# A second place for the state space matrices, and their loads one group ahead

## The chip, the cores and the metric

The kernel runs on one core of a Trainium2 chip. The metric is the device time of one execution, in microseconds (us); the value given for a kernel is the median of its runs. Five engines matter here: TensorE (PE in the profile, its weight loads PEld), VectorE (DVE), ScalarE (ACT), GpSimd (POOL), and SyncE, whose queue (SPq) issues all the DMAs of this kernel, in order.

## The reference, cut to what matters

Two transformer blocks run one after the other on 512 tokens. The second block has two branches from one input projection: an attention branch with compressed, selected and windowed keys, and a state space branch (S5). Only the latter is touched:

```python
def s5_mixer(u, a_re, a_im, log_dt, b_re, b_im, c_re, c_im, d_skip):
    ...
    lam_bar = jnp.exp(lam * dt)
    b_bar = ((lam_bar - 1.0) / lam)[..., None] * lax.complex(b_re.astype(f32), b_im.astype(f32))
    ...
        bu = jnp.einsum('btgc,gpc->btgp', u_chunk.astype(jnp.complex64), b_bar)
        a = jnp.broadcast_to(lam_bar, bu.shape)
        a_cum, b_cum = lax.associative_scan(binop, (a, bu), axis=1)
        s = a_cum * carry[:, None] + b_cum
        y = jnp.real(jnp.einsum('gcp,btgp->btgc', c_mat, s))
    ...
    return y + d_skip.astype(f32) * uf
```

The input u (512 channels in 32 groups of 16) goes through a complex linear recurrence per group and comes back as y. Then y goes through gelu and a gate (glu), and is added to the attention branch by the output projection.

## The kernel before, in words

**The matrices.** Much earlier in the kernel, `s5_params` works the recurrence out for steps of 8 tokens and writes four tables to DRAM: `etd` (input to state), `phd` (phases of the scan), `cld` (state to output) and `tmd` (input to output inside a step). The tokens are then 64 steps of 8.

**The state space stage.** `state_space()` goes over four groups `qb` of 8 channel groups each. `Xs[qb]` holds the inputs of group `qb`, read back from the DRAM tile `ud` to which the projection of u was written (four stores, L1536; the four reads are L1561). For each group there are two halves:

- `states(qb)` loads ET and PH (L1592, L1593), multiplies ET with the inputs on TensorE (L1600, 32 small matmuls in the trace), and makes the states S on VectorE: a rotation by PH, two scans, and a rotation back (L1604 to L1622).
- `loads(qb)` loads CL (two DMAs, L1585) and Tm (L1586). The output half (L1632 to L1642) multiplies Tm with the inputs and CL with the states (L1636, L1637), in two banks of PSUM named tp, copies the result over the inputs (L1640) and stores it to `yd` (L1643).

**Places.** ET, CL and Tm have one place each in SBUF, PH and S have two. A load into a place waits until the last instruction that reads the former contents is done. CL, Tm and ET are 512 KB each, PH is 256 KB, each `Xs[qb]` is 256 KB.

**The order in the program.** `state_space` is a generator. Its steps are woven by hand with those of the rest: the projection `tk1` of the compressed keys (`unit`), and then, in `sides`, the compression of keys and then of values (`cmp_keys`, `cmp_values`) on one side, and `state_space` followed by `kv_tiles` (norm, rotation and transposition of the selected keys, `ks` with the low part `ksl`, and the values `vs`) on the other; between them come the steps of a queue `todo` with the projections `tk2` (queries) and `tk3` (window keys). In program order, `states(qb + 1)` stands before the output half of group qb, and `loads(qb + 1)` behind it.

**What sets the order on the engines.** The program order is a priority only. When the kernel is built, a planner goes through the instructions with estimated times, and puts each one on its engine's queue when its inputs and its place are free by the estimate. On the chip each queue then runs in that order; where an estimate was too short, the engine stands still. So SPq is a sequence in which a DMA that waits for its place holds up those behind it.

**Weights.** Each weight tile is loaded raw (`wraw`, L198, three places), cast on ACT to its high part (`whi`, L208), and subtracted on POOL to its low part (`wlo`, L212); a product is three matmuls (L177 to L179). The compression's weights go the same way (`exraw`, L1788, and `ex`).

Of the kernel before, what the change touches and what calls it, by code (L numbers as in the profile page):

```python
# [13 lines left out]
FT = mybir.dt.float32  # L14
FR = mybir.dt.float32r
# [9 lines left out]
T = 512  # L25
# [102 lines left out]
def turns(*gens):  # L128

    gens = list(gens)  # L130
    while gens:
        for g in list(gens):
            if next(g, gens) is gens:
                gens.remove(g)
            else:
                yield
# [14 lines left out]
def tile_hybrid(ctx: ExitStack, tc: tile.TileContext, I, out):  # L151
    nc = tc.nc
# [355 lines left out]
    with tc.manual_schedule(engines={mybir.EngineType.DVE, mybir.EngineType.Activation, mybir.EngineType.PE}):  # L508
# [68 lines left out]
        for c0, n in ((0, 512), (512, 128)):  # L577
            p = s_ps()
# [138 lines left out]
    for j in range(4):  # L717
        if j < 3:
            paired = index_queries(j + 1)
        st = i_pairs[j]  # L720
# [4 lines left out]
        for i in (1, 2, 3):  # L725
            wd = acc_w[i]
            for e in range(2):
                h = 2 * j + e
                s = (s_ps, tp_ps)[e if j else 0]()
# [93 lines left out]
    for pr in range(2):  # L823
        p = tp_ps()
# [150 lines left out]
    for h in range(4):  # L975
# [39 lines left out]
        while n <= 256:  # L1015
            if n == 1:
                near_weights()
            elif n <= 64:
                s, r = s_ps(), 128 - n
# [6 lines left out]
            elif n == 128:  # L1026
                s = s_ps()
# [4 lines left out]
            else:  # L1032
                s = s_ps()
# [23 lines left out]
        p = tp_ps()  # L1057
# [3 lines left out]
        p = tp_ps()  # L1061
# [100 lines left out]
    L = [small(f"L{i}", (9, 16)) for i in range(2)]  # L1162
# [191 lines left out]
    etd = dr.tile([4, 128, 1024], FT, name="etd")  # L1354
    cld = dr.tile([4, 1024, 128], FT, name="cld")
    phd = dr.tile([4, 128, 512], FT, name="phd")
# [180 lines left out]
    for t in range(NT):  # L1537
        x = XT[:, t]
# [17 lines left out]
    ps5 = sts.enter_context(tc.tile_pool(name="ps5", bufs=1, side="right"))  # L1556
    by_group = lambda v: v.rearrange("(g c) (i j) -> (c i) g j", c=16, i=8)

    Xs = [ps5.tile([128, 8, 64], FT, name=f"X{qb}") for qb in range(4)]
    for qb in range(4):  # L1560
        nc.sync.dma_start(Xs[qb], by_group(ud)[:, 8 * qb:8 * qb + 8])  # L1561

    def cm2(o, a, b, t, conj=False):

# [9 lines left out]
    def state_space():  # L1574

        def st(name, shape, bufs=1):
            return ps5.tile([128] + list(shape), FT, tag=name, bufs=bufs, name=name)


        def loads(qb):  # L1580

            CL, Tm = st("CL", (4, 2, 128)), st("Tm", (8, 128))
            clv = cld[qb].rearrange("(i q e p) x -> i p q e x", i=2, q=4, e=2)
            for i in range(2):
                nc.sync.dma_start(CL[64 * i:64 * i + 64], clv[i])  # L1585
            nc.sync.dma_start(Tm, tmd[qb].rearrange("(g c) (t x) -> (c t) g x", c=16, t=8))  # L1586
            return CL, Tm

        def states(qb):

            ET, PH = st("ET", (4, 2, 128)), st("PH", (2, 4, 64), 2)
            nc.sync.dma_start(ET.rearrange("p q i x -> p (q i x)"), etd[qb])  # L1592
            nc.sync.dma_start(PH.rearrange("p i q j -> p (i q j)"), phd[qb])  # L1593

            bu = tp_ps()
            for q in range(4):
                for e in range(2):
                    for i in range(2):
                        c = i * 256 + q * 64
                        nc.tensor.matmul(bu[64 * e:64 * e + 64, c:c + 64], ET[:, q, i, 64 * e:64 * e + 64],  # L1600
                                         Xs[qb][:, 2 * q + e], start=True, stop=True)

            R8 = st("R8", (4, 64))
            nc.vector.tensor_copy(R8, r8[:, 4 * qb:4 * qb + 4, None].to_broadcast([128, 4, 64]))  # L1604
            nc.vector.memset(R8[:, :, 0:1], 0.0)
            W = [st(f"W{i}", (4, 64)) for i in range(2)]
            tP = t2k()[:, 0:256].rearrange("p (q j) -> p q j", q=4)
            ph = [PH[:, i] for i in range(2)]
            cm2(W, [bu[:, i * 256:(i + 1) * 256].rearrange("p (q j) -> p q j", q=4) for i in range(2)], ph, tP, True)
            for i in range(2):  # L1610
                w = W[i].rearrange("p q j -> p (q j)")
                nc.vector.tensor_tensor_scan(w, R8.rearrange("p q j -> p (q j)"), w, 0.0, op0=OP.mult, op1=OP.add)
            S = st("S", (4, 2, 64), 2)
            nc.vector.memset(S[:, :, :, 0:1], 0.0)
            tS = t2k()[:, 0:504].rearrange("p (i q j) -> p i q j", i=2, q=4)
            wv, pv = [[v[:, :, 0:63] for v in x] for x in (W, ph)]
            for i, op in enumerate((OP.subtract, OP.add)):
                nc.vector.tensor_tensor(tS[:, 0], wv[i], pv[0], op=OP.mult)
                nc.vector.tensor_tensor(tS[:, 1], wv[1 - i], pv[1], op=OP.mult)
                for e in range(2):  # L1620
                    nc.vector.tensor_tensor(S[64 * i:64 * i + 64, :, e, 1:], tS[64 * e:64 * e + 64, 0],
                                            tS[64 * e:64 * e + 64, 1], op=op)  # L1622
            return S

        S, L = states(0), loads(0)
        for qb in range(4):
            yield
            SN = states(qb + 1) if qb < 3 else None
            yield
            CL, Tm = L  # L1630

            for e in range(2):  # L1632
                ys = tp_ps()
                for q in range(4):
                    ov = ys[:, q * 64:(q + 1) * 64]
                    nc.tensor.matmul(ov, Tm[:, 2 * q + e], Xs[qb][:, 2 * q + e], start=True, stop=False)  # L1636
                    nc.tensor.matmul(ov, CL[:, q, e], S[:, q, e], start=False, stop=True)  # L1637
                    if q == 1:
                        yield
                nc.scalar.copy(Xs[qb].rearrange("p (q e) j -> p e q j", e=2)[:, e],  # L1640
                               ys[:, 0:256].rearrange("p (q j) -> p q j", q=4))
                yield  # L1642
            nc.sync.dma_start(by_group(yd)[:, 8 * qb:8 * qb + 8], Xs[qb])  # L1643
            if qb < 3:
                S, L = SN, loads(qb + 1)

    sz = {}

# [17 lines left out]
        nc.scalar.activation(t, o, AF.Tanh, scale=c)  # L1666
        nc.vector.scalar_tensor_tensor(o if dst is None else dst, t, 1.0, x, op0=OP.add, op1=OP.mult)

    p2 = ctx.enter_context(tc.tile_pool(name="p2", bufs=1))
    stp = ExitStack()  # L1670
    pp = stp.enter_context(tc.tile_pool(name="pp", bufs=1))

# [52 lines left out]
    def heads_view(x, c0, b):  # L1725
        return x[:, :, c0:c0 + 64 * b].rearrange("p t (b d) -> p t b d", d=64)

    def kv_tiles(tk, kc0, vc0, tab, name, los):

        kx = heads_view(tk, kc0, 2)  # L1730
        head_norm(kx, 2)
        yield
        rope2(kx, 2, table(tab))
        yield
        ks = []
        for g in range(2):
            k = p2.tile([128, T], FR, name=f"k{name}{g}"), los[:, g]
            kd = t2k().rearrange("p (t e d) -> p t e d", t=NT, e=2)
            for e in range(2):
                nc.scalar.copy(kd[:, :, e], kx[:, :, g])  # L1740
            yield
            p = tp_ps()
            for t in range(NT):
                nc.tensor.transpose(p[:, t * 128:(t + 1) * 128], kd[:, t].rearrange("p e d -> p (e d)"), ident)
            split(p, *k)
            ks.append(k)
        v = p2.tile([128, NT, 2, 128], FR, tag=f"v{name}", bufs=1, name=f"v{name}")
        split(heads_view(tk, vc0, 2), v[:, :, :, 0:64], v[:, :, :, 64:128])
        kvs[name] = ks, v

    kvs = {}

    ssm = state_space()
    tk1, unit = tok_proj(p2, C2["kcr"], 512, tag="tok")

# [92 lines left out]
    def cmp_values():  # L1848
        raws = {k0: cmp_raw("v", k0) for k0 in (0, 4)}
        xb = yield from blocks(128, "v", "szs")  # L1850
        yield
        p, w = yield from compress(xb, "v", "sza", raws)
        pv = p[:, 0:128].rearrange("p (k g n) -> p k g n", k=2, g=2)
        for g in range(2):
            hv = [pp.tile([128, 2, 4, 32], FR, tag=f"hv{i}", bufs=1, name=f"hv{i}") for i in range(2)]
            for k in range(2):
                split(pv[:, k, g, None].to_broadcast([128, 4, 32]), *[v[:, k] for v in hv], scale=0.5)
            yield
            o = s_ps()
            for k in range(2):  # L1860
                mm3(o[:, 0:64], [v[:, k].rearrange("p r n -> p (r n)") for v in hv], [v[:, k] for v in w],
                    k == 0, k == 1)
            vb = vcB[g]
            nc.gpsimd.memset(fl(vb), 0.0)
            for h in range(4):
                r = slice(32 * h, 32 * h + 32)
                split(o[r, 0:64], vb[r, h, 0:64], vb[r, h, 64:128])
            yield
# [10 lines left out]
    tk3, proj3 = tok_proj(pp, C2["kwn"], 256, [(C2["gbr"], 24)])  # L1879
# [4 lines left out]
        yield  # L1884
        head_norm(qv, 8)

    ksl = p2.tile([128, 2, T], FR, name="ksl")
    todo.add(proj2, q_norm(), proj3)
    side_k = cmp_keys()
    for _ in range(3):  # L1890
        some(side_k, 1)
        todo.step()
    sides = turns(chain(side_k, cmp_values()), chain(ssm, kv_tiles(tk1, 256, 384, 0, "s", ksl)))
    for i in range(16):
        some(sides, 3)
        todo.step()
# [38 lines left out]
    nc.scalar.activation(gtv, tk3[:, :, 256:280], AF.Tanh, scale=0.5)  # L1935
    nc.vector.tensor_scalar(gt, gt, 0.5, 0.5, op0=OP.mult, op1=OP.add)
    kwl = p2.tile([128, 2, T], FR, tag="tok", bufs=1, name="kwl")
    sides = turns(cmp_scores(), kv_tiles(tk3, 0, 128, 2, "w", kwl))
    todo.add(silu2("za"), silu2("zs"))
    for _ in range(12):  # L1940
        some(sides, 1)
# [200 lines left out]
```

## Time and profile before

| | |
|---|---|
| three runs | 1318.26, 1321.57, 1322.4 us; median 1321.57 |
| the profiled execution | 1316.25 us |
| its span, first to last instruction | 1314.4 us (1.85 us lie around it) |
| granted TensorE clock, mean | 0.987 |
| busy share of the span | PE 96%, PEld 79%, DVE 62%, POOL 55%, ACT 42% |
| the state space stage in the span | from the first read of the inputs (1013 us) to the last store of `yd` (1101 us) |

Every time below is in us from the span's start. A busy PE is not a PE at its peak, since matmuls are pipelined and their ends are modelled. The trace gives for each engine the time that it stood idle before an instruction, and which event ended it.

### The profile page before, as it was taken

The page shows a single profiled execution, that of the slowest core. Times are in us where ns is not written, and L with a number is a line of the kernel's source. Part 1 is how long each engine was busy: PE and PEld are TensorE (multiplying, and loading weights), DVE is VectorE, ACT ScalarE, POOL GpSimd, SP SyncE. Part 2 cuts the span into 40 slices and gives each one's busy share as a digit, 9 for nine tenths or more (in the row PEclk, how much of TensorE's full clock was granted, in tenths as well). Part 3 has the DMA queues.
Part 4 walks back from the last instruction along what each step waited for, and adds up shares of the span by engine and source line. Part 5 has one row for each costly group of instructions (what it writes and reads, how often), then busy time and mean ns, then how long its engine had stood idle before and what let it go on. Part 6 is the DMA issues. An engine that isn't in the chain of part 4 may idle for free. (4 is left out here: it accounts for less than half of the span.)

```text
span 1314.4 us, 18654 instructions
## 1 busy us (share of the span) xinstructions
PE 1257.2 (96%) x6402; PEld 1034.0 (79%) x6402; DVE 810.0 (62%) x1777; ACT 553.6 (42%) x1258; POOL 727.3 (55%) x923
## 2 busy tenths in 40 slices
PE   8999999999999999999999699999998998989998
PEld 6887887777788888888887588888778887867786
DVE  7765997676533346258667514445257747897885
ACT  5565442232243434252433113433245245658772
POOL 4545544334556465664677446566543385667673
PEclk9999999999999999999999899999999999999999
DMA  7352222221433363332875532543334965222234
GB/s 208 88 151 79 64 71 62 72 57 34 140 88 85 106 172 87 119 90 86 242 208 182 172 119 82 169 132 116 106 102 149 259 185 136 55 91 65 81 105 136
DMA packets 206140, 156.18 MB, mean 119 GB/s; under 512 B 31710, under 2 KB 179882, under 8 KB 206044
## 3 DMA queue, kind: packets, MB, share of 16 engines
q1 hardware_dynamic: 206044, 154.98, 40.3%
q8 instruction: 51, 0.84, 0.3%
q14 instruction: 45, 0.37, 0.1%
HBM read 136.58 MB, written 18.37 MB: 118 GB/s over the span
## 5 line engine op out<-in xcount | busy, mean ns | idle before, releaser
L212 POOL TENSOR_TENSOR wlo<-wraw,whi 128x256 fp32r<-128x256 f32 (+2 forms) x717 | 588.9, 851 | 471.9 <-ACT whi L208 470.4
L208 ACT CAST whi<-wraw 128x512 fp32r<-128x512 f32 (+4 forms) x390 | 212.7, 572 | 353.2 <-PE mm L178 203.2
L177 PE MATMUL mm<-hT,whi 128*128 128x512 f32 (+2 forms) x840 | 331.6, 395 | 0.0
L179 PE MATMUL mm<-hT,wlo 128*128 128x512 f32 (+2 forms) x840 | 325.6, 388 | 0.0
L178 PE MATMUL mm<-hT,whi 128*128 128x512 f32 (+2 forms) x840 | 324.7, 387 | 0.0
L179 PEld LDWEIGHTS mm<-hT,wlo 128*128 128x128 f32 x840 | 158.8, 189 | 30.7
L177 PEld LDWEIGHTS mm<-hT,whi 128*128 128x128 f32 x840 | 158.9, 189 | 28.8 <-ACT whi L208 0.2
L178 PEld LDWEIGHTS mm<-hT,whi 128*128 128x128 f32 x840 | 159.1, 189 | 27.7
L177 PE MATMUL mm<-whi,gT 128*128 128x512 f32 x176 | 71.0, 403 | 13.0 <-DVE t2k L1457 6.9
L1276 DVE TENSOR_TENSOR XT<-XT,mm 128x512 f32<-128x512 f32 x24 | 16.3, 684 | 95.9 <-PE mm L179 95.8
L178 PE MATMUL mm<-wlo,gT 128*128 128x512 f32 x176 | 70.4, 400 | 0.0
L179 PE MATMUL mm<-whi,gT 128*128 128x512 f32 x176 | 70.2, 399 | 0.0
L177 PE MATMUL mm<-whi,hT 128*128 128x512 f32 (+3 forms) x160 | 57.2, 361 | 0.2 <-ACT hT L184 0.2
L179 PE MATMUL mm<-whi,hT 128*128 128x512 f32 (+3 forms) x160 | 56.9, 356 | 0.4 <-DVE hT L185 0.4
L178 PE MATMUL mm<-wlo,hT 128*128 128x512 f32 (+3 forms) x160 | 56.3, 352 | 0.0
L185 DVE TENSOR_TENSOR pt4k<-tp,pt4k 128x512 fp32r<-128x512 f32 (+1 forms) x96 | 46.1, 485 | 15.2 <-ACT pt4k L184 14.5
L184 ACT CAST pt4k<-tp 128x512 fp32r<-128x512 f32 (+1 forms) x96 | 40.0, 421 | 32.9 <-PE tp L398 32.6
L1338 DVE SCALAR_TENSOR_TENSOR am<-aw,prm,am 128x1024 f32<-128x1024 f32 x21 | 29.6, 1408 | 37.7 <-DMA aw<-in_w_ada_dram 37.7
L177 PEld LDWEIGHTS mm<-whi,gT 128*128 128x128 f32 x176 | 33.5, 190 | 23.1 <-DVE t2k L1457 7.3
L187 ACT ACTIVATE gT<-t2k 128x512 fp32r<-128x512 f32 x22 | 13.9, 630 | 78.2 <-DVE t2k L1459 78.2
L179 PEld LDWEIGHTS mm<-whi,gT 128*128 128x128 f32 x176 | 33.6, 191 | 8.3
L178 PEld LDWEIGHTS mm<-wlo,gT 128*128 128x128 f32 x176 | 33.6, 191 | 8.0
(650 smaller groups left out, 2605.9 us busy)
## 6 DMA issues: line engine op xcount, KB each, us to landing
wraw<-in_w_in_dram SPq DMA_DIRECT2D x70, 512.0 KB, 3.8
aw<-in_w_ada_dram SPq DMA_DIRECT2D x24, 512.0 KB, 4.6
wraw<-in_w_ffn_gate_dram SPq DMA_DIRECT2D x22, 512.0 KB
wraw<-in_w_ffn_up_dram SPq DMA_DIRECT2D x22, 512.0 KB, 4.5
wraw<-in_w_ffn_down_dram SPq DMA_DIRECT2D x20, 512.0 KB, 3.8
wraw<-in_w_out_dram SPq DMA_DIRECT2D x16, 512.0 KB, 3.8
PA<-biasd SPq DMA_DIRECT2D x4, 640.0 KB, 5.9
x<-in_x_dram SPq DMA_DIRECT2D x4, 512.0 KB, 4.5
```

Of the source, the lines that this page charges most:

```text
L177: nc.tensor.matmul(o, a[0], b[0], start=first, stop=False)
L178: nc.tensor.matmul(o, a[0], b[1], start=False, stop=False)
L179: nc.tensor.matmul(o, a[1], b[0], start=False, stop=last)
L184: nc.scalar.copy(hi, p)
L185: return nc.vector.tensor_tensor(lo, p, fl(hi), op=OP.subtract)
L187: nc.scalar.activation(hi, p, AF.Copy, scale=scale)
L208: nc.scalar.copy(hi[:, d], raw[:, d])
L212: low_at[0] = nc.gpsimd.tensor_tensor(lo[:, e], raw[:, e], fl(hi[:, e]), op=OP.subtract)
L1276: nc.vector.tensor_tensor(XT[:, t, n0:n0 + 512], XT[:, t, n0:n0 + 512], o, op=OP.add)
L1338: nc.vector.scalar_tensor_tensor(am, aw, cs[:, k:k + 1], am, op0=OP.mult, op1=OP.add)
```

## The change

- ET and PH of group 0 are loaded in front of the four reads of the inputs, no longer behind them.
- ET and PH of group qb + 1 are asked for right behind the ET matmuls of group qb (they were asked for at the start of `states(qb + 1)`). The places are as before: one for ET, two for PH.
- CL and Tm of the odd groups get places of their own, in the pool p2: those of `ksl` and `vs`, which `kv_tiles` fills once the state space is done. `loads(qb + 1)` now stands right behind `states(qb + 1)`, in front of the output half of group qb.
- So that this can be, p2 is opened earlier, and `ksl` is allocated at the start of `kv_tiles`.

```diff
     Xs = [ps5.tile([128, 8, 64], FT, name=f"X{qb}") for qb in range(4)]
+    def state_loads(qb):
+        ET = ps5.tile([128, 4, 2, 128], FT, tag="ET", bufs=1, name="ET")
+        PH = ps5.tile([128, 2, 4, 64], FT, tag="PH", bufs=2, name="PH")
+        nc.sync.dma_start(ET.rearrange("p q i x -> p (q i x)"), etd[qb])
+        nc.sync.dma_start(PH.rearrange("p i q j -> p (i q j)"), phd[qb])
+        return ET, PH
+
+    first_loads = state_loads(0)
     for qb in range(4):
         nc.sync.dma_start(Xs[qb], by_group(ud)[:, 8 * qb:8 * qb + 8])
+    p2 = ctx.enter_context(tc.tile_pool(name="p2", bufs=1))
...
         def loads(qb):
-            CL, Tm = st("CL", (4, 2, 128)), st("Tm", (8, 128))
+            if qb % 2:
+                CL = p2.tile([128, 4, 2, 128], FT, tag="ksl", bufs=1, name="CL")
+                Tm = p2.tile([128, 8, 128], FT, tag="vs", bufs=1, name="Tm")
+            else:
+                CL, Tm = st("CL", (4, 2, 128)), st("Tm", (8, 128))
...
         def states(qb):
-            ET, PH = st("ET", (4, 2, 128)), st("PH", (2, 4, 64), 2)
-            nc.sync.dma_start(ET.rearrange("p q i x -> p (q i x)"), etd[qb])
-            nc.sync.dma_start(PH.rearrange("p i q j -> p (i q j)"), phd[qb])
+            ET, PH = due[qb]
...
+            if qb < 3:
+                due[qb + 1] = state_loads(qb + 1)
...
+        due = {0: first_loads}
         S, L = states(0), loads(0)
         for qb in range(4):
             yield
-            SN = states(qb + 1) if qb < 3 else None
+            if qb < 3:
+                SN, LN = states(qb + 1), loads(qb + 1)
...
             if qb < 3:
-                S, L = SN, loads(qb + 1)
+                S, L = SN, LN
...
     def kv_tiles(tk, kc0, vc0, tab, name, los):
+        los = los()
...
-    ksl = p2.tile([128, 2, T], FR, name="ksl")
...
-    sides = turns(chain(side_k, cmp_values()), chain(ssm, kv_tiles(tk1, 256, 384, 0, "s", ksl)))
+    sides = turns(chain(side_k, cmp_values()), chain(ssm, kv_tiles(tk1, 256, 384, 0, "s", lambda: p2.tile([128, 2, T], FR, tag="ksl", bufs=1, name="ksl"))))
```

## Rows read from the trace of the kernel before

**Rows 1.** The page: busy time, share of the span, instructions.
```profile
PE 1257.2 (96%) x6402; PEld 1034.0 (79%) x6402; DVE 810.0 (62%) x1777; ACT 553.6 (42%) x1258; POOL 727.3 (55%) x923
```

**Rows 2.** Busy time by stretch; in brackets instructions; last granted clock, DMA share, GB/s.
```profile
1000.00:1085.00 85.00, 84.71 (x612) 73.72 (x611) 50.68 (x108) 31.87 (x64) 44.23 (x60) 1.00 0.75 218
1016.00:1034.00 18.00, 18.00 (x117) 14.54 (x118) 8.64 (x19) 3.18 (x5) 8.75 (x13) 1.00 0.87 225
1034.00:1044.00 10.00, 9.81 (x108) 8.50 (x106) 8.58 (x20) 3.02 (x6) 4.50 (x6) 1.00 0.91 256
...
1090.00:1092.00 2.00, 2.00 (x10) 1.68 (x10) 0.47 (x2) 1.05 (x3) 0.00 (x0) 0.59 0.96 189
1092.00:1094.00 2.00, 2.00 (x11) 2.00 (x11) 1.94 (x4) 2.00 (x7) 0.79 (x2) 0.55 0.01 2
1114.00:1120.00 6.00, 5.77 (x36) 5.44 (x37) 4.83 (x9) 3.73 (x10) 3.66 (x5) 0.72 0.00 0
1120.00:1165.00 45.00, 43.09 (x226) 35.45 (x225) 40.32 (x74) 25.41 (x59) 30.09 (x31) 1.00 0.33 94
```

**Rows 3.** All waits of PE from 1005 to 1135: total us, times, longest.
```profile
PE s L178 <- POOL ex L212: 3.4, 4, 2.5
PE tp L1636 <- DMA Tm<-tmd: 2.8, 1, 2.8
PE tp L1600 <- DMA ET<-etd: 0.2, 1, 0.2
```

**Rows 4.** Timeline of PE: start, us, instruction, in brackets idle before and releaser.
```profile
1022.25 1.20 PE L1600 MATMUL tp<-X,ET 128*64 128x64 f32 x32
...
1040.62 1.17 PE L1600 MATMUL tp<-X,ET 128*64 128x64 f32 x32 [0.19 <-DMA ET<-etd]
...
1089.84 0.41 PE L1636 MATMUL tp<-X,Tm 128*128 128x64 f32 x2 [2.80 <-DMA Tm<-tmd]
...
1099.22 0.60 PE L1773 MATMUL tp<-ident,t2k 128*128 128x128 f32 x4
...
1112.15 0.33 PE L178 MATMUL s<-ex,xb 128*64 128x256 f32 x1 [2.53 <-POOL ex L212]
...
1168.51 0.33 PE L419 MATMUL s<-ks,qst 128*128 128x128 f32 x1 [4.77 <-DVE qst L188]
```

**Rows 5.** Timeline of SPq: issues of DMAs (time in the queue, waits included).
```profile
1013.14 0.39 SPq L1561 DMA_DIRECT2D X<-ud  x1
...
1017.19 0.58 SPq L1592 DMA_DIRECT2D ET<-etd  x1
...
1034.81 0.32 SPq L1592 DMA_DIRECT2D ET<-etd  x1
...
1041.45 0.62 SPq L1586 DMA_DIRECT2D Tm<-tmd  x1
1042.17 3.14 SPq L198 DMA_DIRECT2D wraw<-in_w_in_dram  x3
...
1057.55 0.64 SPq L1586 DMA_DIRECT2D Tm<-tmd  x1
1058.24 0.79 SPq L1592 DMA_DIRECT2D ET<-etd  x1
...
1084.57 0.46 SPq L1586 DMA_DIRECT2D Tm<-tmd  x1
```

**Rows 6.** Timeline of DVE, as in rows 4.
```profile
1016.41 0.39 DVE L1912 TENSOR_SCALAR nm<-cm 128x128 f32<-128x128 f32 x1 [4.60 <-DMA x2d<-XT]
1025.59 0.42 DVE L1566 TENSOR_TENSOR W<-tp,PH 128x256 f32<-128x256 f32 x1 [8.78 <-DMA PH<-phd]
...
1057.40 1.06 DVE L185 TENSOR_TENSOR vs<-tok,vs 128x512 fp32r<-128x512 f32 x1
```

**Rows 7.** Timeline of ACT, as in rows 4.
```profile
1050.89 0.62 ACT L208 CAST whi<-wraw 128x512 fp32r<-128x512 f32 x1
...
1086.19 0.41 ACT L1769 COPY t2k<-tok 128x256 f32<-128x256 f32 x1
```

More of the change, by code (lines that the diff above doesn't have):

```diff
@@ L1667, in gelu2 @@
         nc.vector.scalar_tensor_tensor(o if dst is None else dst, t, 1.0, x, op0=OP.add, op1=OP.mult)
-    p2 = ctx.enter_context(tc.tile_pool(name="p2", bufs=1))
     stp = ExitStack()
@@ L1937, in tile_hybrid @@
     kwl = p2.tile([128, 2, T], FR, tag="tok", bufs=1, name="kwl")
-    sides = turns(cmp_scores(), kv_tiles(tk3, 0, 128, 2, "w", kwl))
+    sides = turns(cmp_scores(), kv_tiles(tk3, 0, 128, 2, "w", lambda: kwl))
     todo.add(silu2("za"), silu2("zs"))
```

## The prediction

> **What bounds the kernel now.** I began with the busy times of the whole page: PE is the fullest engine by far [rows 1]. Whoever wants to know what a change in one stage is worth must then ask that stage, so I took the busy times by stretch. From 1000 to 1085, which holds nearly all of the state space stage, PE is busy 84.71 of 85 us at full clock, DVE and DMA are not full [rows 2]. There a DMA that lands earlier gives nothing unless PE waits for it. The list of all waits of PE between 1005 and 1135 is short [rows 3]: 2.8 us for Tm, 0.2 us for an ET, 3.4 us for weights that POOL splits. The timeline of PE puts the Tm wait at 1087 to 1089.84 [rows 4], and the timeline of the DMA queue shows why: that Tm, of group 3, was issued at 1084.57 [rows 5], behind the last use of the only place, and landed some 5 us later. Behind the wait the granted clock was 0.59 and 0.55 for two stretches of 2 us, that is mostly the lower of the two levels [rows 2]. The second wait, for POOL, is followed by a clock of 0.72 over 6 us [rows 2]. After that PE and DVE are both nearly full until 1165: 43.09 and 40.32 of 45 us.
>
> So the stage holds about 3.4 + 2.8 + 0.2 = 6.4 us of PE idle time, and some 3.4 us lost to the clock: (1 - 0.59) x 2 + (1 - 0.55) x 2 = 1.7 us behind the Tm wait, (1 - 0.72) x 6 = 1.7 us behind the other. No more than 9.8 us can be had from PE here.
>
> **The change part by part.**
>
> *Tm and CL of group 3.* Their new place is free when the output half of group 1 is done. The Tm of group 2 took over group 1's old place at 1057.55 [rows 5], so that half was done by then; group 2's own half ends only just before 1084.57. Asked for at 1058 and 5 us under way, Tm is some 27 us ahead of its use at 1089.84. The wait goes, and with it the clock's fall: 2.8 + 1.7 = 4.5 us. The ET of group 2, for which PE waited 0.19 us at 1040.62 [rows 4], is asked for at the same moment as before: ET still has one place, and the matmuls that free it stand where they stood. I take its 0.2 us neither as gain nor as loss.
>
> *ET and PH of group 0 in front of the inputs.* ET was issued at 1017.19, and PH after it, behind inputs that are asked for from 1013.14 on [rows 5]. The first ET matmul ran at 1022.25 [rows 4], and DVE stood 8.78 us until PH landed at 1025.59 [rows 6]. Both can now go some 4 to 6 us earlier, and with them the DVE work of groups 0 to 2. What hides this gain is PE, busy 18.00 of 18 us from 1016 to 1034 with projections [rows 2], and a DVE that has much spare time up to 1085 (busy 50.68 of 85 us). Price 0. In exchange the first inputs come behind 768 KB: at the 225 GB/s of this stretch 3.5 us. The matmuls of 1022.25 did not wait for them; if they had landed only just in time, PE would now stand 3.5 us. But they were issued 4 us ahead of the ET of the same matmuls and are half as large, so I take the lower end, 0.
>
> *ET and PH of group 3* move from 1058.24 to about 1042, right behind the ET matmuls of group 2. PE was full at both times, so: 0.
>
> *CL and Tm of group 1* move from about 1041 to soon after 1023.4, where the ET matmuls of group 0 end, and those of group 2 from the time up to 1057.55 to about 1041 [rows 4, 5]. The new place lies on memory that the outputs of the first block leave: DVE's wait for the store of x2d ended at 1016.41 [rows 6], seven us before the load, so no wait from that side. These are 1 MB earlier in a stretch in which DMA was 0.87 busy; from 1034 to 1044 it was 0.91 [rows 2]. Everything issued behind them lands later until the backlog has drained: the ET of group 2 (issued at 1034.81) and the three weight tiles of tk2 (1042.17) [rows 5], whose first cast ran at 1050.89 [rows 7]. The lower bound is 0, if there is slack; the upper is the full time of what stands in front, worked out under the rivals. The nearest row is the ET wait, 0.2 us in a stretch just as crowded; since more is loaded there now I take 1.0 us.
>
> *vs and ksl as lodgings.* Before, ACT and DVE filled `vs` at 1057, in a gap. Now `vs` is free only after group 3. The DVE instruction (1.06 us [rows 6]) moves into the stretch in which DVE has 40.32 of 45 us [rows 2]: 0 if it finds one of the remaining gaps, 1.1 if not. I take 1.1 us. `ksl` was filled behind the state space before as well: 0.
>
> *What comes behind.* The compression of the values needs a tp bank for its transpositions. Its first input copy was done at 1086.6 [rows 7], the transposition ran at 1099.22 [rows 4]: the two banks were with group 3's output half, which waited for Tm and CL. With group 3 early, this chain can start up to some 10 us earlier, while PE gets only 4.5 us earlier, so PE should still have projections to run when POOL splits the weights for which it waited from 1109.6 on [rows 4]. That can close the second hole (3.4 + 1.7 = 5.1 us), or leave it, since POOL's order (weights of the gate, then rotation, then these weights) is set by the planner. Between 0 and 5.1 I take the middle, 2.5 us.
>
> *The sum.* -4.5 - 2.5 + 1.1 + 1.0 = -4.9 us. On the profiled execution's own time, 1316.25 us (span 1314.4 and 1.85 around it), that is 1311.3. The median of the runs is 1321.57, 5.3 us above that execution; the same step from it gives 1316.7 us. A measurement of this kernel tells about 0.3% from no change, here 4.0 us.
>
> **The rivals.**
>
> *1. The wait goes and nothing is won.* Behind 1092, DVE is nearly as full as PE, and PE comes to a gap of 4.77 us before 1168.51 all the same [rows 4]. If the chain through DVE and POOL sets the end of this part, PE's gain turns into a longer wait at one of the two. For it: DVE's 40.32 of 45 us. Against it: DVE and ACT stood idle too, behind PE's Tm wait (busy 0.47 and 1.05 of the 2 us from 1090), so their chain moves up as well. Then: 0 to -3.5 us, about 1319.8. The same time comes out if the planner, with loads that it believes earlier, merely orders things anew.
>
> *2. Slower: the loads moved forward are paid for by those behind them.* The place is PE at 1040 to 1056, the first product of tk2 and the ET matmuls of group 2. In front of tk2's weights there now stand CL and Tm of group 1 as backlog (1.05 MB at 256 GB/s: 4.1 us) and, if they are issued first, ET and PH of group 3 (0.79 MB: 3.1 us), together 7.2 us. If the weights have no slack, PE stands 7.2 us and loses 1.7 us to the clock, as behind the Tm wait: 8.9 - 4.5 + 1.1 = +5.5 us, 1327.1. It decides from a stall of about 3.4 us on, where the gain is gone. For it: DMA is 0.9 busy there. Against it: PE waited for no weights there, and there are small products of the state space to run meanwhile. The Trainium skill (DMA: Bandwidth & Descriptors, Two DMAs through the same engine are not ordered) says that descriptors of one queue start in order; by that rule everything issued behind the moved loads does start later. The trace agrees so far that the ET issued at 1034.81 was the one that came late.
>
> *3. More is won.* The second hole closes altogether, `vs` finds a gap and no load is late: -4.5 - 5.1 = -9.6, 1312.0; with the DVE chain earlier still, somewhat less.
>
> **How the numbers follow.** Forecast, between -4 and -8 us (1313.5 to 1317.5, the likeliest at 1316.7): 0.42. Rival 3: 0.12. Rival 1, within 4 us of before: 0.29. Rival 2, more than 4 us slower: 0.17. Faster by over 0.3% is forecast and rival 3, 0.54; within 0.3% 0.29; slower 0.17. The range is 1309.5 to 1326.0. Below it lies some 0.05, in rival 3: its lower end is all of PE's idle time and clock loss (9.8 us: 1311.8) and the 2.1 us that PH of group 0 landed behind the matmuls of group 0 (1025.59 against 1023.4), which DVE could hand on (1309.7). Above it lies most of rival 2, some 0.13: its upper end is that rival's 1327.1 less 1.0 us of slack, about 1326.
>
> **What would show it.** Right: no wait of L1636 for Tm; the Tm of group 3 issued before 1065; the clock at 1.00 where it was 0.59 and 0.55; the cast and subtraction into `vs` behind 1080; PE idle from 1005 to 1135 about 3 us instead of 6.4. The forecast is wrong if PE waits for `whi` or ET between 1020 and 1056 (rival 2), if the wait for POOL's `ex` has grown or PE's gap before 1168.51 is longer by as much as was won (rival 1), or if this wait is gone too (rival 3). If L1600 of group 0 waits for X, the inputs paid for the first loads.

## The result and the profile after

The changed kernel took 1329.51 us (median of 5 runs, 1328.82 to 1334.1), the kernel before 1321.35 us (5 runs, 1314.92 to 1322.4): ratio 1.0073 [1.0052, 1.0095]. That is slower: by 8.2 us between the medians, by about 9.6 us by the ratio. The forecast was -4.9 us, and the time lies above the range.

The line of the page that answers to [rows 1]:

```profile
PE 1263.0 (95%) x6402; PEld 1038.4 (78%) x6402; DVE 813.2 (61%) x1777; ACT 553.2 (42%) x1258; POOL 726.7 (55%) x923
```

The work is the same; the span went from 1314.4 to 1327.7 us. Some 2.8 of these 13.3 us lie ahead of the first instruction that the change moves (a weight load of SPq at 990.12 before is at 992.88 after, and the store to `ud` at 1012.24 is at 1015.03), so they belong to the two executions; 10.5 are left to explain. A time of after less 2.8 can be held against a time of before. Busy times by stretch, of after:

```profile
1050.00:1060.00 10.00, 7.90 (x51) 6.46 (x52) 2.28 (x7) 4.98 (x11) 1.79 (x3) 0.94 0.99 308
1060.00:1070.00 10.00, 8.30 (x52) 7.20 (x49) 9.27 (x15) 5.57 (x10) 8.54 (x10) 0.50 0.33 91
1070.00:1080.00 10.00, 10.00 (x48) 8.40 (x47) 4.33 (x6) 1.24 (x2) 7.74 (x10) 0.88 0.82 207
1080.00:1110.00 30.00, 30.00 (x198) 26.88 (x196) 10.89 (x35) 16.70 (x45) 19.88 (x36) 1.00 0.47 129
1110.00:1130.00 20.00, 14.73 (x90) 12.31 (x89) 17.32 (x33) 7.69 (x16) 10.78 (x14) 0.84 0.30 79
1130.00:1180.00 50.00, 45.46 (x242) 37.87 (x240) 42.19 (x79) 28.22 (x64) 34.29 (x36) 0.98 0.34 95
```

and the last three of the same stretches before (from 1050 to 1080 PE was busy 10.00 of 10 us three times, at 1.00):

```profile
1080.00:1110.00 30.00, 26.82 (x186) 24.44 (x184) 18.58 (x52) 15.64 (x41) 15.70 (x27) 0.94 0.58 153
1110.00:1130.00 20.00, 16.98 (x96) 14.07 (x97) 15.44 (x33) 12.86 (x38) 13.45 (x18) 0.91 0.20 53
1130.00:1180.00 50.00, 44.61 (x219) 36.69 (x218) 47.64 (x89) 27.97 (x58) 32.77 (x33) 0.97 0.29 85
```

The loss of a stretch is PE's idle time plus its busy time by what the clock lacks of 1.00. From 1050 to 1080 that is 3.79 us idle and 0.06 x 7.90 + 0.50 x 8.30 + 0.12 x 10 = 5.8 us of clock: 9.6 us, where before had nothing. From 1080 to 1110 the loss went from 3.18 + 1.61 = 4.8 us to nothing: that is the Tm wait, gone as forecast. From 1110 to 1130 it grew from 4.6 to 7.6 us. With 0.6 us more from 1008 to 1050 and 1.4 us more from 1130 to 1230 the sum is 9.6 - 4.8 + 3.1 + 0.6 + 1.4 = 9.9 of the 10.5 us. (The clock is given in hundredths, so a sum can be off by some tenths of a us.) A new hole appeared some 30 us ahead of the one that was closed.

The longest waits of PE from 1005 to 1135, after; they answer to [rows 3]:

```profile
PE s L178 <- POOL ex L212: 2.9, 1, 2.9
PE mm L178 <- POOL wlo L212: 1.7, 1, 1.7
PE s L177 <- ACT xb L184: 1.1, 1, 1.1
PE tp L1790 <- ACT t2k L1786: 1.1, 1, 1.1
PE tp L1613 <- issue: 1.0, 1, 1.0
PE tp L1613 <- DMA ET<-etd: 0.8, 1, 0.8
```

Tm is not among them. `wlo` is new: PE waits for POOL's weights of tk2. The 3.79 us idle from 1050 to 1080 are three gaps (PE, after):

```profile
1057.05 1.27 PE L1790 MATMUL tp<-ident,t2k 128*128 128x128 f32 x8 [1.07 <-ACT t2k L1786]
1059.34 2.00 PE L1613 MATMUL tp<-X,ET 128*64 128x64 f32 x32 [1.02 <-issue]
...
1068.99 0.80 PE L178 MATMUL mm<-wlo,hT 128*128 128x512 f32 x1 [1.70 <-POOL wlo L212]
```

Only the last of them is a wait for POOL. The first two fall where PE before ran tk2's product (L177 to L179, from 1052.41) and now has none of it to run; for the second the trace names no releaser. The clock falls behind these two, ahead of the wait for `wlo` (the last section has the rows).

The timeline of SPq, after (ET is now L1564, PH L1565, CL L1600, Tm L1601, the store to yd L1660, exraw L1805), answers to [rows 5]:

```profile
1035.33 0.82 SPq L1601 DMA_DIRECT2D Tm<-tmd  x1
1042.39 0.38 SPq L1660 DMA_DIRECT2D yd<-X  x1
1043.12 0.33 SPq L1564 DMA_DIRECT2D ET<-etd  x1
1043.54 0.40 SPq L1565 DMA_DIRECT2D PH<-phd  x1
1043.99 1.27 SPq L1600 DMA_DIRECT2D CL<-cld  x2
1045.31 0.62 SPq L1601 DMA_DIRECT2D Tm<-tmd  x1
1045.98 4.72 SPq L1805 DMA_DIRECT2D exraw<-in_cmp_w_k_dram  x2
1050.80 2.30 SPq L198 DMA_DIRECT2D wraw<-in_w_in_dram  x3
...
1070.03 0.99 SPq L1601 DMA_DIRECT2D Tm<-tmd  x1
```

From 1036.2 to 1042.4 SPq issues nothing: it stands at the store of group 0 (6.2 us, waiting for ACT's copy). Behind the store come group 3's ET and PH and group 2's CL and Tm, 1.75 MB, and only then the two `exraw`, the first weights of the key compression, and tk2's three `wraw`. Before, the `exraw` had gone out one by one at 1033.76 and 1035.18, ahead of that store, and the `wraw` at 1042.17, 2.5 us behind it (SPq, before):

```profile
1035.18 0.43 SPq L1788 DMA_DIRECT2D exraw<-in_cmp_w_k_dram  x1
1039.65 0.37 SPq L1643 DMA_DIRECT2D yd<-X  x1
```

The wait at the store is not new: SPq stood 4.0 us at it before, and less the 2.8 us it goes out at the same moment (1039.6). New is what stands behind it. The two `exraw` also take 4.72 us to issue (0.44 and 0.43 before, one by one); why, the trace does not say. POOL, before and after:

```profile
1038.40 3.03 POOL L212 TENSOR_TENSOR ex<-exraw,ex 128x256 fp32r<-128x256 f32 x4 [7.79 <-ACT ex L208]
1042.53 3.46 POOL L212 TENSOR_TENSOR ex<-exraw,ex 128x256 fp32r<-128x256 f32 x4 [1.09 <-ACT ex L208]
1051.59 8.86 POOL L212 TENSOR_TENSOR wlo<-wraw,whi 128x256 fp32r<-128x256 f32 x12 [5.60 <-ACT whi L208]
```

```profile
1058.21 2.78 POOL L212 TENSOR_TENSOR ex<-exraw,ex 128x256 fp32r<-128x256 f32 x4 [25.03 <-ACT ex L208]
1062.44 4.57 POOL L212 TENSOR_TENSOR ex<-exraw,ex 128x256 fp32r<-128x256 f32 x4 [1.46 <-ACT ex L208]
1066.97 10.15 POOL L212 TENSOR_TENSOR wlo<-wraw,whi 128x256 fp32r<-128x256 f32 x12
```

Before, POOL split `ex` while PE still ran tk1, and was free when tk2's weights came. After, it stands 25 us with nothing to do, and then the `ex` and the `wlo` fall due together: tk2's first `wlo` begins at 1066.97 instead of 1051.59. PE runs out of tk1 meanwhile. Not all of this is POOL's: tk2's first `whi`, without which no `wlo` can begin, is cast on ACT at 1062.79, against 1050.89 before [rows 7], and no wait for its load is recorded there; it stands on ACT behind the casts of `ex` and `xb`. How much of its delay is the late issue and how much the order that the planner gave ACT, no run separates.

```profile
1062.79 1.14 ACT L208 CAST whi<-wraw 128x512 fp32r<-128x512 f32 x2
```

### The profile page after: what moved, and what is told of

The parts are those of the page before. It is cut to its first block, busy times and chain, and to the rows that moved or that the text cites. A ratio compares the mean times of both kernels' runs of the same rounds, so it can differ in the third digit from the quotient of the medians.

```text
span 1327.7 us, 18655 instructions
## 1 busy us (share of the span) xinstructions
PE 1263.0 (95%) x6402; PEld 1038.4 (78%) x6402; DVE 813.2 (61%) x1777; ACT 553.2 (42%) x1258; POOL 726.7 (55%) x923
## 5 line engine op out<-in xcount | busy, mean ns | idle before, releaser
L177 PE MATMUL mm<-hT,whi 128*128 128x512 f32 (+2 forms) x840 | 331.5, 395 | 0.0
L179 PE MATMUL mm<-hT,wlo 128*128 128x512 f32 (+2 forms) x840 | 324.8, 387 | 0.0
L179 PEld LDWEIGHTS mm<-hT,wlo 128*128 128x128 f32 x840 | 158.6, 189 | 30.9
L177 PEld LDWEIGHTS mm<-hT,whi 128*128 128x128 f32 x840 | 158.9, 189 | 29.4 <-DVE sza L1674 0.4
L177 PE MATMUL mm<-whi,gT 128*128 128x512 f32 x176 | 70.9, 403 | 12.4 <-DVE t2k L1457 6.3
L179 PE MATMUL mm<-whi,gT 128*128 128x512 f32 x176 | 70.2, 399 | 0.0
L177 PE MATMUL mm<-whi,hT 128*128 128x512 f32 (+3 forms) x160 | 58.3, 367 | 0.1
L179 PE MATMUL mm<-whi,hT 128*128 128x512 f32 (+3 forms) x160 | 57.8, 361 | 0.4 <-DVE hT L185 0.4
L177 PEld LDWEIGHTS mm<-whi,gT 128*128 128x128 f32 x176 | 33.5, 190 | 22.5 <-DVE t2k L1457 6.7
L212 POOL TENSOR_TENSOR ex<-exraw,ex 128x256 fp32r<-128x256 f32 x32 | 24.5, 801 | 30.3 <-ACT ex L208 30.3
L179 PEld LDWEIGHTS mm<-whi,gT 128*128 128x128 f32 x176 | 33.4, 190 | 8.2
```

The lines of the kernel that those rows point to most:

```text
L177: nc.tensor.matmul(o, a[0], b[0], start=first, stop=False)
L179: nc.tensor.matmul(o, a[1], b[0], start=False, stop=last)
L212: low_at[0] = nc.gpsimd.tensor_tensor(lo[:, e], raw[:, e], fl(hi[:, e]), op=OP.subtract)
```

## The experiments

Theories. **M**: the moved matrices hold up the issue queue, and the weights of the key compression and of tk2 behind them come too late for POOL; what counts is the order. **R**: the moved bytes compete for DMA bandwidth, whatever the order. **F**: the first ET and PH in front of the inputs delay the first states. Each of the 12 kernels was compared with the kernel before on the same chip; the medians of before were 1320.67, 1321.37 and 1319.03 us in the three groups of four. Each edit went through the planner again, so its effect holds whatever the planner reordered on the other engines; no run holds that order fixed.

**One part alone.** `e2_states_ahead`: only ET and PH as in the change. `e4_places_only`: only the second place, and CL and Tm asked for early. `e3_loads_late`: the whole change, but CL and Tm asked for where the kernel before does it:

```diff
-                SN, LN = states(qb + 1), loads(qb + 1)
+                SN = states(qb + 1)
...
-                S, L = SN, LN
+                S, L = SN, loads(qb + 1)
```

> Only ET and PH of the change (in front of the inputs, and one group ahead); CL and Tm in one place as before. M: the first exraw goes ahead of the store of yd again, the second one behind CL, Tm, ET and PH: a part of the loss, 1321 to 1326, with the Tm wait of 2.8 us back. R: 1323 to 1327. F: 1326 to 1331.

> Only CL and Tm of the change: odd groups in p2 and asked for behind states(qb + 1); ET and PH as before. M: exraw is still issued behind CL and Tm of groups 1 and 2 and behind the first store of yd, so nearly all of the loss stays: 1326 to 1331. R: half of the moved bytes, so half of the loss: 1323 to 1327. F: the loss goes and the Tm wait with it: 1316 to 1319.

> The change, but CL and Tm asked for at the old point of the program, behind the output half (places of the odd groups kept). M: exraw still stands behind CL and Tm of group 1, the store of yd, and ET and PH of group 3: 1323 to 1330; the wait for the Tm of group 3 is gone. R: as M less 1 to 3. F: 1328 to 1331.

Measured: e2 1324.86 us, 1.0039 [1.0023, 1.0055]; e4 1330.8 us, 1.0082 [1.0059, 1.0106]; e3 1323.72 us, 1.0031 [1.0011, 1.0050]. In e4, without any ET or PH in front, SPq issues the `exraw` at 1044.05 and the `wraw` at 1047.15, and of PE's longest waits those for `wlo` and `whi` are new:

```profile
PE mm L178 <- POOL wlo L212: 4.2, 1, 4.2
PE s L178 <- POOL ex L212: 2.9, 1, 2.9
PE mm L177 <- ACT whi L208: 1.9, 1, 1.9
```

So CL and Tm alone cost as much as the whole change, and F is not its cause. ET and PH alone cost about half. e4 lies in M's range and not in R's; e2 and e3 lie in both and don't tell the two apart. In e2 the first `exraw` goes out ahead of the store of `yd`, as M said, the second one at 1048.76 behind CL, Tm, ET and PH, and SPq's longest wait from 1025 to 1052 is 5.9 us at the CL of group 1, whose place is still read. The parts don't add up; that they hold up the same loads is read from this order, not tried.

**The first loads alone, and the place alone.** `e1_first_only` asks only for the first ET and PH in front of the inputs; `e5_second_place` has only the second place, with every load asked for where the kernel before asks.

> The kernel before with only the first group's ET and PH asked for in front of the inputs. M: nothing is moved past the weights, so the time stays within 2 us of before. If loads in front of the inputs delay the inputs and with them the first states (F): 1323 to 1325.

> The kernel before with the second place for CL and Tm alone: every load is asked for where the kernel before asks for it. M: the key-compression weights and the next projection's weights are issued behind at most one moved group, the Tm wait of the last groups goes in part, and the time is 1318 to 1323. R: with two places the matrices of group 1 still move about 10 us earlier than before, so contention would leave 1324 or more.

Measured: e1 1318.89 us, 0.9986 [0.9966, 1.0005]; e5 1321.16 us, 0.9992 [0.9971, 1.0013]. Neither costs anything that can be told from no change. F falls, and the second place is harmless by itself: it is the asking ahead that costs. In e5 the wait for Tm is gone too, and no gain can be told. Its trace also limits M: the `exraw` went out at 1043.68 there, some 7.6 us later than before (its store to `ud` is 2.4 us later, at 1014.59), and POOL stood 16.7 us; but tk2's `wraw` went out at 1045.00, only 0.5 us later by the same count, and PE waited 1.1 us for `wlo`. So late `exraw` alone cost little.

**The weights in front.** `e6_exraw_front` is the changed kernel with the first two `exraw` asked for in front of the state space; `e11_both_front` asks there for tk2's first two weight loads too, into tk2's own tile:

```diff
+    key_raws = {k0: cmp_raw("k", k0) for k0 in (0, 4)}
+    tk2 = p2.tile([128, NT, 512], FT, tag=f"tok{C2['q']}", bufs=1, name="tok")
+    q_raws = {k: q_raw(k) for k in (0, 2)}
     ssm = state_space()
```

> The changed kernel with one more edit: the first two loads of the key compression's weights (exraw) are asked for ahead of the state space stage. Theory M (order on the issue queue: the matrices moved forward stand ahead of exraw, POOL idles 25 us and then splits exraw and tk2's weights in one bunch): POOL's idle time of 25.0 us goes, PE no longer waits near 1055 to 1072, and most of the 4.6 us idle and 6.8 us of lost clock there come back: 1318 to 1322 us, 8 to 11 below the changed kernel. Rival R (the DMA engines are full, so the same bytes earlier delay all others in any order): ET or CL come later instead, and the time stays at 1326 to 1331. Rival F (ET and PH in front of the inputs delay the first states): no change from the changed kernel, 1328 to 1331.

> The changed kernel with both late loads in front of the state space: the first two key-compression weights, and the first two weight loads of the next projection (into that projection's own output tile, which is written only at its end). All state space loads stay where the change puts them. Order on the issue queue (M): TensorE no longer waits for weights between 1050 and 1075 us, its busy time there is above 9 of 10, and the time is 1316 to 1321, no slower than the kernel before. Contention for DMA bandwidth (R): the same bytes move in the same stretch and even earlier, so the time stays at 1326 or more, as with the key-compression weights alone in front (1326.7).

Measured: e6 1326.72 us, 1.0044 [1.0023, 1.0064]; e11 1323.15 us, 1.0001 [0.9983, 1.0019]. In e6 the `exraw` went out at 1024.33 and 1026.08, but tk2's `wraw` only at 1048.22, and PE was still busy only 7.91 us of 1050 to 1060; that is a smaller return than M had expected of the `exraw` alone, and the time lies in R's range. POOL's idle time did not go but moved: it split `ex` early and then stood 25.2 us until tk2's `wlo`. The wait for `wlo` is gone, the gaps of 1.07 and 1.02 us are still there, and the clock from 1060 to 1070 is 0.50 as in the changed kernel. With both in front the new hole is gone; the time is 2.2 us above M's range, and no slower than the kernel before, as M said (e11, busy times by stretch):

```profile
1030.00:1040.00 10.00, 10.00 (x46) 8.27 (x45) 7.29 (x14) 4.47 (x8) 7.40 (x9) 1.00 1.08 328
1040.00:1050.00 10.00, 10.00 (x88) 8.73 (x86) 7.95 (x13) 1.51 (x3) 9.20 (x12) 1.00 1.15 255
1050.00:1060.00 10.00, 10.00 (x87) 8.81 (x86) 8.42 (x25) 4.42 (x10) 0.00 (x0) 1.00 0.96 219
1060.00:1070.00 10.00, 10.00 (x63) 8.78 (x62) 4.23 (x10) 3.79 (x7) 1.86 (x3) 1.00 0.63 188
...
1080.00:1110.00 30.00, 28.55 (x203) 26.02 (x202) 23.57 (x54) 17.64 (x48) 19.34 (x33) 1.00 0.49 127
1110.00:1130.00 20.00, 16.01 (x90) 13.32 (x89) 12.58 (x30) 9.59 (x27) 10.22 (x15) 0.83 0.20 54
1130.00:1180.00 50.00, 44.34 (x215) 36.56 (x214) 45.91 (x84) 27.64 (x59) 33.86 (x34) 0.93 0.34 95
```

The DMA engines are about as full as the changed kernel's (a share of 1.08 and 1.15 from 1030 to 1050, there 1.17 and 0.92), and PE loses nothing for it. R falls as it was put (whatever the order): all moved loads are still moved, and in another order the same bytes cost nothing that can be told.

**Who holds the queue.** `e8_store_act` has the stores to yd issued by ACT; `e15_matrices_act` has all matrices of groups 1 to 3 issued by ACT:

```diff
-            nc.sync.dma_start(by_group(yd)[:, 8 * qb:8 * qb + 8], Xs[qb])
+            nc.scalar.dma_start(by_group(yd)[:, 8 * qb:8 * qb + 8], Xs[qb])
```

```diff
-        nc.sync.dma_start(ET.rearrange("p q i x -> p (q i x)"), etd[qb])
+        (nc.scalar if qb else nc.sync).dma_start(ET.rearrange("p q i x -> p (q i x)"), etd[qb])
```

> The changed kernel with the four stores of the state space output issued by ScalarE instead of SyncE, behind the copy that they wait for anyway. M with the store as the block: the 6.2 us for which the first store holds the issue queue go, the key-compression weights are issued some 6 us earlier, and the time is 1321 to 1325. M with the matrices of the next groups as the block (they wait for the tiles that the same group's matmuls still read): they hold the queue in the store's place, and the time stays at 1327 to 1331. R: 1327 to 1331 too, with the weights issued early.

> The changed kernel with the state space matrices of groups 1 to 3 (ET, PH, CL, Tm) issued by ScalarE instead of SyncE; the same bytes, the same tiles, the same waits. M (queueing): SyncE issues the key-compression weights and the next projection's weights by about 1040 us, GpSimd is busy between 1035 and 1058 again, TensorE is busy for over 9 of 10 us in 1050 to 1070, and the time comes back to 1318 to 1323, or to 1326 at most if ScalarE, which now stands behind the waiting loads in SyncE's place, is late with its casts. R (bandwidth): 1327 or more.

Measured: e8 1333.15 us, 1.0068 [1.0041, 1.0095]; e15 1324.82 us, 1.0045 [1.0030, 1.0060]. In e8 SPq stands just as long, now at the ET of group 3, whose only place is read by matmuls of 1043.90 to 1045.10 (SPq):

```profile
1037.81 0.62 SPq L1601 DMA_DIRECT2D Tm<-tmd  x1
1045.13 0.33 SPq L1564 DMA_DIRECT2D ET<-etd  x1
...
1048.08 3.37 SPq L1805 DMA_DIRECT2D exraw<-in_cmp_w_k_dram  x2
```

So the store was only the first of two that wait for about the same moment. The time lies above all ranges given for it; the 1333.15 us can't be told from the changed kernel's by their ratios. In e15 the `exraw` go out at 1031.78 and the first two `wraw` at 1036.39, PE is busy 10.00 of 10 us at 1.00 in each slice from 1040 to 1080, and `wlo` is no longer waited for. The hole of the change is gone by another queue alone. But the planner put CL of group 0 between the reads of the inputs, and the early states pay: PE waits 2.8 us for X and 2.4 us for ET at L1613. That puts it within M's range and not back at the kernel before; that these two waits are the rest of its loss is argued from the trace, not tried.

**Where the gain went.** With the hole mended (e11) the forecast's gain does not show either. Theory **H**: the wait for POOL's `ex` of the value compression around 1110 to 1130 takes it back. Three kernels have the low half of one of these four parts made by DVE instead of POOL: `e17_before_low_dve` on the kernel before, `e16_place_low_dve` on e5, `e18_both_low_dve` on e11:

```diff
-                low_at[0] = nc.gpsimd.tensor_tensor(lo[:, e], raw[:, e], fl(hi[:, e]), op=OP.subtract)
+                if low:
+                    low.tensor_tensor(lo[:, e], raw[:, e], fl(hi[:, e]), op=OP.subtract)
+                    continue
+                low_at[0] = nc.gpsimd.tensor_tensor(lo[:, e], raw[:, e], fl(hi[:, e]), op=OP.subtract)
...
+                       nc.vector if n == "v" and k0 in (8,) else None)
```

> The same split on VectorE in the kernel before, its state space loads untouched. H: the wait for Tm (2.8 us) is still there, so 0 to 2.5 us below the kernel before. The other: the same as with the second place.

> The second place for CL and Tm alone (1321.2, equal to before), and the low half of the third part of the value-compression weights split by VectorE instead of GpSimd. If the gain of the Tm wait was taken back by the wait for those weights around 1110 to 1130 (H): the wait gets shorter by some 2 us, and this kernel is 2 to 6 us below the kernel before, by more than the same edit on the kernel before. If the gain never was one (TensorE's wait for Tm covered by something else): this kernel and the same edit on the kernel before come out alike, within 1.5 us.

> The changed kernel with both late loads in front (1323.2, ratio 1.0001) and the same split on VectorE. H: 2 to 6 us below the kernel before, as with the second place. The other: as the kernel before, within 2 us.

Measured: e17 1318.16 us, 0.9992 [0.9981, 1.0003]; e16 1317.42 us, 0.9994 [0.9980, 1.0008]; e18 1316.14 us, 0.9979 [0.9970, 0.9989]. Only e18 is clearly below the kernel before, by 2.8 us; its interval overlaps those of e11, e16 and e17. The wait for `ex` did go in e16 and e18, and one of 3.0 us for `t2k` came; the one for `qst` was there before [rows 4] (waits of PE from 1005 to 1180 in e18, the longest; in e16 the same two are 4.7 and 3.0):

```profile
PE s L422 <- DVE qst L188: 4.8, 1, 4.8
PE tp L1766 <- ACT t2k L1762: 3.0, 1, 3.0
```

In e17 it did not go: PE waits 4.2 us for `ex` there, now made by DVE, so e17 is a poor control for the other two. H foresaw e18 and missed e16, which comes out like e17, as the other theory said. H is not shown. What the rows of e11 above do show is the place: from 1080 to 1110 the loss fell from 4.8 to 1.45 us, and from 1110 to 1180 it rose from 4.55 + 6.73 = 11.3 to 6.71 + 8.76 = 15.5 us (idle time and clock, worked out as above). The sizes depend on where the stretches are cut: e11's execution lies 5.3 us later (store to `ud` at 1017.50), and stretches moved by as much give 3.2 and 14.0 us. Which chain sets the end of that stretch stays open. e18 is the version whose time is the lowest.

## Why the prediction was wrong

**The step that failed** is the last one on CL and Tm of groups 1 and 2: "since more is loaded there now I take 1.0 us". Alone, this part costs 0.82%, some 10.8 us (e4), with the gain of the Tm wait already taken off. Two things were missed in it. First, what stands behind the moved loads: I named the ET of group 2 and tk2's weights, but not the two `exraw`, though they go out at 1033.76 and 1035.18 in the kernel before, right in the stretch that I read. Their lateness moves POOL's split of `ex` from a time when POOL is free to the time when tk2's weights are due. Of the loss, e6 returns some 3.8 us (1.0073 to 1.0044, with intervals that overlap) and e11, with tk2's weights in front too, another 5.7 us (to 1.0001, clear of e6's); judged by e5 and e6, the late weights of tk2 weigh more than the late `exraw`. Secondly, the nearest row was taken from the wrong kind of cost: the ET wait of 0.2 us was a transfer in a crowded stretch, while the price here is a place on the queue: the `exraw` now stand behind the store at which SPq stands until its data is ready, and the `wraw` behind 1.75 MB of matrices and the `exraw` (issued at 1050.80, 5.8 us later than before once the 2.8 us are taken off).

**ET and PH of the next group** were put at 0, because PE was full at both times. With the first ones in front they cost 0.39% (e2): "PE was full at both times" left out what is issued behind them, there the second `exraw` (1048.76) and tk2's weights (1049.51). The first ET and PH in front of the inputs, also put at 0, cost nothing that can be told (e1).

**Rival 2** (0.17) was the case that came. Its time was 1327.1, against 1329.51 measured; its stall with the clock was 8.9 us, against 9.6 us read from 1050 to 1080. That the two sums come so close is in part luck: it put 7.2 us on the stall and 1.7 us on the clock, and measured were 3.8 and 5.8. (The 3.4 us from which it was to decide count stall and clock together; by its own sum the stall alone is 1.7 us.) Its place was 1040 to 1056, and it came later, since PE lives on tk1 until 1055; its releaser was to be the weights of tk2: of the 3.79 us idle, 1.70 are a wait for `wlo`, and 2.09 two gaps in which tk2's product is missing. Its signs came in part: PE waited 0.8 us for an ET, and was idle 10.0 us from 1005 to 1135, against 6.4 before and 3 forecast. The mechanism was right except for its middle: not the bytes in front (7.2 us by bandwidth; e11 moves them and loses nothing), but the order on the queue and, behind it, the late work of ACT and POOL. The rule quoted there, that descriptors in one queue start in order (Trainium skill, DMA: Bandwidth & Descriptors, Two DMAs through the same engine are not ordered), is about descriptors on a queue of one DMA engine, and no row here shows when those start. What the trace shows is the step before, the issue on SyncE: the first `exraw` behind the moved loads went from 1033.76 to 1045.98. The bound that I worked out beside the rule was the bandwidth's; what SPq waits for ahead of a load was not counted.

**The clock** was mis-sized. I took 1.7 us for each hole; from 1050 to 1080 it cost 5.8 us, more than the idle time itself (3.8 us).

**The Tm wait** went, as forecast, and the clock from 1080 to 1110 is 1.00. The Tm of group 3 was issued at 1070.03, not before 1065, still 21 us ahead of its use (L1653 at 1091.47). The subtraction into `vs` went behind 1080 (1115.29, 1.02 us) as forecast; its own price of 1.1 us was not measured.

**The second hole** was to shrink by 2.5 us. It stayed (2.9 us at POOL's `ex`) and cost more than before. Even with the new hole mended the forecast fails: e11, at 1.0001 [0.9983, 1.0019], has no room for -4.9 us (0.9963), nor has e5 at 0.9992 [0.9971, 1.0013]. That is rival 1, which decides once rival 2 is out of the way: the wait goes and next to nothing is won.

## What to carry to other kernels

A load asked for earlier on an in-order issue queue is not free because its transfer is hidden. List every DMA behind its new position, and ask how long the queue's head will wait there for a place or for data; then follow the weights that come late to the engines that prepare them, since an engine idle now may have its work bunched later. Here the earlier loads were free once the loads that the nearer work needs went first (e11), but they won nothing by themselves. A wait removed from the fullest engine need not shorten the kernel (e5, e11); that another chain bounds the stretch behind it is the likely reason, and is not shown.

## What was not expected of the hardware

The clock stayed low while PE was full again. In the changed kernel PE was busy 1.92 of 4 us from 1056 to 1060, then had no idle time until the wait for `wlo` that ended at 1068.99, and none behind it; the granted clock was at the lower of its two levels from 1060 to 1072, and 0.95 from 1072 to 1076 (after; start and end, busy times, clock):

```profile
1056.00:1060.00 4.00, 1.92 (x20) 1.52 (x22) 2.28 (x7) 2.63 (x7) 1.79 (x3) 0.84 0.78 287
1060.00:1064.00 4.00, 4.00 (x39) 3.88 (x35) 3.37 (x8) 3.13 (x5) 2.54 (x3) 0.50 0.41 123
1064.00:1069.00 5.00, 3.30 (x14) 2.49 (x13) 4.93 (x7) 2.44 (x5) 5.00 (x7) 0.50 0.14 25
1069.00:1072.00 3.00, 3.00 (x7) 2.44 (x8) 2.92 (x5) 0.00 (x0) 3.00 (x4) 0.50 1.11 315
```
